# Moving squares of x and weight staging to later blocks in a planned matrix product on one core

## The chip, the cores and the metric

One core of a Trainium2 chip runs the whole program. The metric is device time in microseconds (us) of one execution; the time given for a kernel is the median of its runs. Five engines take instructions in their own order: TensorE (PE), VectorE (DVE), ScalarE (ACT), GpSimd (POOL) and SyncE (SP). POOL, SP and, at the start and the end, ACT also issue DMA transfers.

## The reference

```python
batch, m, k, h, n = 16, 512, 768, 3072, 768      # x, w1, b1, w2 are float32
y = np.maximum(np.matmul(x, w1) + b1, 0)
return np.matmul(y, w2).astype(np.float32)
```

So 8192 rows of x go through a 768 to 3072 layer with bias and relu, and then through a 3072 to 768 layer.

## The kernel before

The rows are cut into 8 blocks of 1024 (`NSB`), the 3072 hidden columns into two halves (`NCH`). An iteration `it` takes one block through one half: `it` 0 to 7 are the first pass over the blocks with the first half of w1 and w2, `it` 8 to 15 the second pass. The second pass begins with the block that ended the first one (`block`), and adds its result to what the first pass has stored in the output: POOL's DMA stores accumulate.

Each iteration has a first stage, the product of x and w1 (`add_first`, matmuls at L924), and a second stage, the product of y and w2 (`add_second`, matmuls at L1045). Both use a bilinear scheme with fewer products than the plain one: 20 products replace 24 in each of the two column groups of the first stage, 20 replace 24 in the second. The price is sums of inputs on DVE: of x (`X_SUMS`, L674), of w1 (`W1_SUMS`, L690, over both column groups `g` at once), of y (L897) and of w2 (`W2_SUMS`, L712). It also costs operations behind the products: they are kept as sums in `s`, seed another PSUM bank, or go out. In the first stage these are on ACT (L954, L958) and DVE (L961, L964, L970), in the second on ACT (L1057) and DVE (L1060). Block 0 alone has a plain first product (`first_block`, L834), since its weights' sums aren't there yet; its first rows are turned by PE.

The second stage makes eight outputs per block, each in one of the four buffers `o`, and stores each as 384 KB. Normally an output with a kept sum `u` is added to it on DVE. In the iterations named in `APART` it is not: ACT copies the output alone, SP stores the kept sum (L1093, in the first pass), and POOL's accumulating store (L1090) adds the output to it in DRAM.

x reaches `xn` by a POOL load with a cast to fp16 (L571, two halves of 768 KB per block), and SP's DMA transposes (L625, eight per block) bring it into `x`. In the last iteration the free slots of `x` hold what the first pass stored (`prior`, L1019); POOL adds the kept sums to it (L1098), and DVE then adds the product.

The fast scheme is only used for data in a known range, so the kernel sums squares of all inputs: of x in place in `xn` after the transposes (L633, ACT), of block 0's first four row tiles from `o` (L1197), of w1 (L728) and w2 (L742). `add_check` compares them in the second pass; a general path follows if they are out of range.

The weights of the second half are staged by POOL into DRAM in fp16, in the first pass: six strips of w1 (L553, `w1d`) and twelve of w2 (L559, `w2d`), three per iteration from `it` 1 on. SP loads them when pass 1 ends.

The order on every engine is made before the program runs, by `Graph.run`: each step is a task with an engine, a cost in ns, a latency and the data it reads and writes. PE's order is the order in which its tasks are added. The other engines take, of what can start, the task with the earliest due time, worked out backward from the PE task that needs it. Tasks marked `idle`, all squares among them, go into gaps that the plan shows. `take` picks the PSUM bank, kept-sum slot or output buffer. On the chip each engine then runs its list strictly in order and waits at each step for what that step reads or overwrites.

```python
self.g.add("ACT", 1030, square, writes=[("xn", s), ("stat", "x", i)], due=due, idle=True)   # add_square_x
to = it + 2 + (it + 2 == NSB)      # iteration_end: the block after the next is loaded into xn
```

Of the kernel before, what the change touches and what calls it, by code (L numbers as in the profile page):

```python
# [14 lines left out]
ACTF = mybir.ActivationFunctionType  # L15
# [215 lines left out]
class Graph:  # L231
# [65 lines left out]

        return self.places["ps"][i ^ 1][0] <= start

    def take(self, reg, start):  # L300

        p = self.places[reg.kind]
        if reg.kind == "ps":
            if reg.seeded:
                found = sorted((max(f, start), self.spare(i, start), -full, i)
                               for i, (f, full) in enumerate(p)
                               if full >= (2 if reg.seeded == 2 else 1))
            else:
                found = sorted((max(f, start), self.spare(i, start), full, i)
                               for i, (f, full) in enumerate(p))  # L310
            if reg.n == 2:
                at = {i: f for f, _, _, i in found}
                found = sorted((max(f, at[i + 1]), i) for i, f in at.items()
                               if i % 2 == 0 and i + 1 in at)
                if not found or found[0][0] > 1e8:
                    return None
                f, i = found[0]
                return f, [i, i + 1]
            if not found or found[0][0] > 1e8:
                return None  # L320
            return found[0][0], [found[0][3]]
        best = None
        step = reg.n if reg.kind == "s" else 1
        for i in range(0, len(p) - reg.n + 1, step):
            f = max(p[k][0] for k in range(i, i + reg.n))
            if f < 1e8 and (best is None or f < best[0]):
                best = (f, list(range(i, i + reg.n)))
        return best

    def run(self, begin=0.0, lookahead=0.2, ahead=5):  # L330
# [6 lines left out]
        for t in reversed(self.tasks):  # L337
# [4 lines left out]
            due = t.late = late  # L342
# [5 lines left out]
        product = {}  # L348
        for t in self.tasks:
            if t.engine == "PE":  # L350
                for r in t.regs:
                    product.setdefault(r, t.pe)
        avail = {e: [] for e in self.ENGINES}
        free = {e: begin for e in self.ENGINES}
        order, head, drift, left = [], 0, 0.0, len(self.tasks)
# [11 lines left out]
        while left:  # L367
            best = None
            for e in self.ENGINES:
                cands = []  # L370
                low = 1e9
                for t in avail[e]:
                    if e == "PE" and t.pe != head:
                        continue
                    start = max(free[e], t.ready)
                    if start > low + lookahead:
                        continue
                    ok = True
                    for r in t.regs:
                        if r.at is None:  # L380
                            if e != "PE" and r.kind == "ps" and r in product:
                                if product[r] > head + ahead:
                                    ok = False
                                    break
                            got = self.take(r, start)
                            if got is None:
                                ok = False
                                break
                            start = max(start, got[0])
                    if not ok:  # L390
                        continue
                    if t.idle and start < t.due + drift:
                        d = demand[e]
                        while first[e] < len(d) and d[first[e]].end is not None:
                            first[e] += 1
                        if first[e] < len(d) and start + t.ns > d[first[e]].late + drift + 0.3:
                            continue
                    cands.append((start, t))
                    low = min(low, start)
                if cands:  # L400
                    start, t = min((c for c in cands if c[0] <= low + lookahead),
                                   key=lambda c: (c[1].due, c[1].n))
                    if best is None or (start, t.n) < best[:2]:
                        best = (start, t.n, t, e)
# [50 lines left out]

APART = (0, 7)

STATS = ((1, 2, 3, 4, 5, 6, 7), (2, 3, 4))  # L460


class Fast:
# [153 lines left out]
        return x[:, :, (s % 2) * P:(s % 2 + 1) * P]  # L617

    def add_load_x(self, it, half):
        self.g.add("POOL", 760, lambda: self.load_x(it, half), lat=9.0,  # L620
                   writes=[("xn", 4 * half + s) for s in range(4)])

    def add_turns(self, it):
# [3 lines left out]
                writes=[("x", 2 * (s // 2) + k, s % 2) for k in range(2)])  # L627

    def add_square_x(self, it, s, due=None):
        i = it * 8 + s  # L630

        def square():
            self.nc.scalar.activation(out=self.xn[:, s, :], in_=self.xn[:, s, :],  # L633
                                      func=ACTF.Square,
                                      accum_out=self.stat[:, self.stat_at["x"] + i:][:, 0:1])
        self.g.add("ACT", 1030, square, writes=[("xn", s), ("stat", "x", i)], due=due, idle=True)
# [43 lines left out]

    def add_w1_sums(self):

        for o, i, j, sign in W1_SUMS:
            a, b, d = (self.w1s[q] for q in (o, i, j))

            def add(a=a, b=b, d=d, sign=sign):
                w = self.v1.rearrange("p g a k h -> p g a (k h)")
                self.nc.vector.tensor_tensor(out=w[:, :, a], in0=w[:, :, b], in1=w[:, :, d],  # L690
                                             op=ALU.add if sign > 0 else ALU.subtract)
            self.g.add("DVE", 950, add,
                       reads=[("w1", g, q) for g in range(2) for q in (b, d)],
                       writes=[("w1", g, a) for g in range(2)])

    def add_w2_signs(self, c):
        for i in W2_NEG:
# [2 lines left out]
                out=self.v2[:, a], in_=self.v2[:, a], func=ACTF.Copy, scale=-1.0),  # L700
                writes=[("w2", a, s) for s in range(4)])

    def add_w2_sums(self, c, parts):
        slot = self.w2s[c]
        for n, (o, i, j, sign) in enumerate(W2_SUMS):
            a, b, d = (slot[q] for q in (o, i, j))
            for s0 in range(0, 4, 4 // parts):
                s1 = s0 + 4 // parts

# [313 lines left out]
    def add_second(self, it):  # L1023
# [71 lines left out]
                **({"accum_op": ALU.add} if c else {}))  # L1095

        def add_prior(to, u, b):
            nc.gpsimd.tensor_tensor(out=self.prior(to), in0=self.prior(to), in1=sum_of(kept[u]),  # L1098
                                    op=ALU.add if b > 0 else ALU.subtract)

        where = {p: ch for ch, chain in enumerate(SECOND_CHAINS) for k, p in chain if k == "m"}
        for kind, n in steps:
# [14 lines left out]
            if what == "out":  # L1117
                dest = Reg("o")
                if final:
                    engine = "DVE"  # L1120
                    if u is not None:
                        self.g.add("POOL", 1850, lambda to=to, u=u, b=b: add_prior(to, u, b),
                                   reads=self.prior_keys(to) + [kept[u]],
                                   writes=self.prior_keys(to))
                    reads += self.prior_keys(to)
                elif u is not None and apart:
                    assert b == 1
                    self.g.add("POOL" if c else "SP", 1375 if c else 100,
                               lambda to=to, u=u: store_sum(to, u), reads=[kept[u]],
                               writes=[("out", self.block(it), to)], lat=6.5)  # L1130
                    engine = "ACT"
                elif u is not None:
                    reads.append(kept[u])
# [12 lines left out]
            if what == "out" and not (final and n == last):  # L1146
# [1 line left out]
                self.g.add("SP" if plain else "POOL", 100 if plain else 1375,  # L1148
                           lambda to=to, dest=dest, plain=plain: store(to, dest, plain),
                           reads=[dest],  # L1150
                           writes=[("out", self.block(it), to)], lat=6.5)

# [37 lines left out]
    def plan(self):  # L1192
        g, NSB, NIT = self.g, self.NSB, self.NIT
        self.presets()
        for s in range(4):
            def square(s=s):
                self.nc.scalar.activation(out=self.junk, in_=self.o[:, s],  # L1197
                                          func=ACTF.Square,
                                          accum_out=self.stat[:, self.nsum + s:][:, 0:1])
            self.first_rows = getattr(self, "first_rows", [])  # L1200
            self.first_rows.append(square)
        self.hold = [g.held(Reg("o"), [s]) for s in range(4)]
        self.first_block()
        for s in range(4):
            g.add("ACT", 1030, self.first_rows[s], reads=[("rows", s), self.hold[s]],
                  writes=["junk", ("stat", "x", s)], idle=True, due=24.0)
        for s in range(4):
            self.add_square_x(0, 4 + s)
        self.add_stats(0, False, second=False)
        self.add_w2_signs(0)  # L1210
        self.add_stats(0, False, first=False)
        self.add_w2_sums(0, 2)
        self.add_w1_sums()
        self.add_load_x(1, 1)
        self.iteration_end(0)
        later = None
# [10 lines left out]
    def iteration(self, it):  # L1227
# [6 lines left out]
        if it == NSB - 1:  # L1234
# [4 lines left out]
                    reads=[("w1d", gi, h) for h in range(3)],  # L1239
                    writes=[("w1", gi, a) for a in range(6)])  # L1240
            self.add_stats(1, False, second=False)
            self.add_w1_sums()
        if it <= 6:
            for n in range((it - 1) * 3, it * 3):
                gi, h = divmod(n, 3)
                if n < 6:
                    g.add("POOL", 850, lambda gi=gi, h=h: self.load_strip(self.w1dram, 1, gi, h),
# [6 lines left out]
    def iteration_end(self, it):  # L1254
# [4 lines left out]
        self.add_second(it)  # L1259
        if it + 1 < NIT and it + 1 != NSB:  # L1260
            self.add_turns(it + 1)
            if it + 1 < NSB:
                for s in range(8):
                    self.add_square_x(it + 1, s)
            to = it + 2 + (it + 2 == NSB)
# [4 lines left out]
        if it == NSB - 1:  # L1270
# [6 lines left out]
                    writes=[("w2", slot[i], s) for s in range(4)])  # L1277
            self.add_w2_signs(1)
            self.add_stats(1, False, first=False)
            self.add_w2_sums(1, 2)  # L1280

    def build(self):
        self.place_all()
# [62 lines left out]
```

## Time and profile before

| | us |
|---|---|
| median of 3 runs | 875.39 |
| lowest and highest | 875.18, 876.65 |
| the profiled execution: its time | 876.98 |
| the profiled execution: its span, first to last instruction | 875.3 |
| PE busy in it | 855.2 |
| DVE, ACT, POOL busy | 686.8, 478.9, 143.2 |
| mean granted clock of TensorE | 0.994 |

The profile is of one execution. A row of the page or of an answer names the line of the kernel, the engine, the operation and what it writes and reads. Idle time is given with what ended it, as `[3.38 <-DMA out_dram<-o]`: the engine had been idle for 3.38 us when a store of `o` let it go on. In the list of waits the three numbers are us in total, times, and the longest. In a table of stretches each row has the stretch, its length, and the busy time of PE, PEld (weight loads, which run beside matmuls), DVE, ACT and POOL with their instructions, then TensorE's granted clock, the share of the 16 DMA engines and GB/s. An SP or POOL row that issues a transfer lasts as long as the issue; its landing is told apart.

### The profile page before, as it was taken

How to read it: one execution, taken by the hardware profiler on the slowest of the kernel's cores; microseconds unless marked ns; L12 is line 12 of the kernel's file. 1: busy time of each engine (PE TensorE's matmuls, PEld its weight loads, DVE VectorE, ACT ScalarE, POOL GpSimd, SP SyncE). 2: the span in 40 equal slices, each digit the busy share in tenths (PEclk: the TensorE clock that was granted, in tenths of full speed). 3: DMA queues.
4: the chain of work that ended last, by engine and by line, in shares of the span. 5: the costliest groups of instructions: out<-in, count | busy, mean ns of one | idle time of the engine just before them, and what ended most of it. 6: DMA issues, size and time to landing. Idle time of an engine off the chain costs nothing.

```text
span 875.3 us, 16234 instructions
## 1 busy us (share of the span) xinstructions
PE 855.2 (98%) x6445; PEld 635.0 (73%) x6445; DVE 686.8 (78%) x1023; ACT 478.9 (55%) x951; POOL 143.2 (16%) x155
## 2 busy tenths in 40 slices
PE   8998799999999999999999999999999999999996
PEld 8556568778686776868678686877868677686873
DVE  2787497887879788797999979788786978869774
ACT  6876456757476583654755253664737435253350
POOL 5213010100101001000030402213031130402204
PEclk9999899999999999999999999999999999999998
DMA  9979977484835649372698868779586886963743
GB/s 211 192 162 207 132 135 168 89 214 74 184 106 107 165 73 243 59 159 74 232 211 136 128 102 126 116 126 151 105 122 106 133 127 109 139 98 55 127 145 127
DMA packets 162978, 119.85 MB, mean 137 GB/s; under 512 B 93244, under 2 KB 161364, under 8 KB 162644
## 3 DMA queue, kind: packets, MB, share of 16 engines
q0 software_dynamic: 49760, 58.99, 44.3%
q1 hardware_dynamic: 112672, 58.81, 27.5%
q8 instruction: 51, 0.84, 0.4%
q10 hardware_dynamic: 468, 1.00, 0.3%
q14 instruction: 27, 0.22, 0.1%
HBM read 73.94 MB, written 59.77 MB: 153 GB/s over the span
## 4 chain that ended last, share of the span: by engine, by line
PE 88%; DMA 4%; issue 4%; DVE 1%; POOL 1%; ACT 1%; SPq 0%; POOLq 0%; DVEq 0%; ACTq 0%
PE ps L924 42%; PE ps L1045 42%; PE ps L834 4%; DMA out_dram<-o 1%; DMA x<-xn 1%; POOL x L1098 1%; DMA out_dram<-s 1%; DVE v L690 1%; PE ps L776 1%; DMA o<-in_x_dram 1%; DVE s L1060 0%; DMA x<-out_dram 0%; ACT s L958 0%; DVE ps L1060 0%; ACT junk L728 0%
## 5 line engine op out<-in xcount | busy, mean ns | idle before, releaser
L1045 PE MATMUL ps<-v,y 128*128 128x384 f16 x2560 | 419.3, 326 | 1.1 <-DVE o L1060 0.6
L924 PE MATMUL ps<-x,v 128*128 128x256 f16 x3600 | 398.5, 273 | 10.0 <-ACT ps L958 6.1
L924 PEld LDWEIGHTS <-v 128*128 128x128 f16 x3600 | 353.1, 98 | 54.4 <-issue 11.1
L1045 PEld LDWEIGHTS <-y 128*128 128x128 f16 x2560 | 250.4, 98 | 165.8 <-issue 2.0
L961 DVE CUSTOM_DVE_ANT_0 y<-ps,s 128x512 f16<-128x512 f32 x240 | 161.4, 688 | 72.7 <-PE ps L924 53.7
L897 DVE TENSOR_TENSOR y<-y 128x1024 f16<-128x1024 f16 (+2 forms) x227 | 165.6, 755 | 8.7 <-ACT y L843 6.2
L958 ACT ACTIVATE s<-ps,bt 128x256 f32<-128x256 f32 x180 | 73.8, 472 | 109.9 <-PE ps L924 106.6
L1090 POOL DMA_DIRECT2D out_dram<-o x68 | 81.8, 1297 | 201.3 <-DVE o L1060 68.3
L674 DVE TENSOR_TENSOR x<-x 128x768 f16<-128x768 f16 (+1 forms) x168 | 109.5, 684 | 0.5
L571 POOL DMA_DIRECT2D xn<-in_x_dram x30 | 22.7, 758 | 474.1 <-ACT xn L633 303.3
L1057 ACT ACTIVATE ps<-ps 128x768 f32<-128x768 f32 x48 | 38.2, 795 | 108.9 <-PE ps L1045 90.4
L1057 ACT ACTIVATE s<-ps 128x768 f32<-128x768 f32 x64 | 51.7, 809 | 61.9 <-PE ps L1045 61.3
L958 ACT ACTIVATE y<-ps,bt 128x256 f16<-128x256 f32 x180 | 73.6, 471 | 20.2 <-PE ps L924 18.4
L633 ACT ACTIVATE xn<-xn 128x768 f16<-128x768 f16 x60 | 50.2, 838 | 9.5 <-DMA x<-xn 9.3
L1060 DVE TENSOR_TENSOR o<-ps,s 128x768 f32<-128x768 f32 x52 | 49.1, 954 | 7.5 <-PE ps L1045 4.1
L1057 ACT ACTIVATE o<-ps 128x768 f32<-128x768 f32 x42 | 33.9, 808 | 21.5 <-PE ps L1045 13.5
L1060 DVE TENSOR_TENSOR s<-ps,s 128x768 f32<-128x768 f32 x32 | 30.6, 956 | 14.3 <-PE ps L1045 13.7
L970 DVE TENSOR_TENSOR s<-s,ps 128x512 f32<-128x512 f32 x30 | 20.5, 684 | 20.1 <-PE ps L924 20.1
L958 ACT ACTIVATE ps<-ps,bt 128x256 f32<-128x256 f32 x60 | 26.9, 448 | 17.1 <-PE ps L924 8.1
L954 ACT ACTIVATE ps<-ps 128x512 f32<-128x512 f32 x60 | 35.0, 584 | 0.7
L834 PE MATMUL ps<-x,v 128*128 128x256 f16 (+1 forms) x216 | 31.9, 308 | 0.3 <-DVE x L784 0.3
L1060 DVE TENSOR_TENSOR o<-s,ps 128x768 f32<-128x768 f32 x26 | 24.7, 950 | 7.8 <-DMA out_dram<-o 6.8
(63 smaller groups left out, 367.6 us busy)
## 6 DMA issues: line engine op xcount, KB each, us to landing
out_dram<-o POOLq DMA_DIRECT2D x68, 384.0 KB, 6.8
out_dram<-o SPq DMA_DIRECT2D x59, 384.0 KB, 6.0
xn<-in_x_dram POOLq DMA_DIRECT2D x28, 768.0 KB, 8.3
out_dram<-s SPq DMA_DIRECT2D x12, 384.0 KB, 8.2
x<-out_dram SPq DMA_DIRECT2D x8, 384.0 KB, 3.4
v<-in_w_dram POOLq DMA_DIRECT2D x6, 384.0 KB, 9.1
v<-in_w_dram POOLq DMA_DIRECT2D x12, 192.0 KB, 10.1
w1d<-in_w_dram POOLq DMA_DIRECT2D x6, 384.0 KB, 14.7
```

Of the source, the lines that this page charges most:

```text
L633: self.nc.scalar.activation(out=self.xn[:, s, :], in_=self.xn[:, s, :], func=ACTF.Square, accum_out=self.stat[:, self.stat_at["x"] + i:][: ...
L674: self.nc.vector.tensor_tensor(out=self.two(x, out), in0=self.two(x, in0), in1=self.two(x, in1), op=ALU.add if sign > 0 else ALU.subtract)
L834: nc.tensor.matmul(self.ps[:, ps.at[0], cols], lhsT=self.v1[:, gi, 2 * h + k2, k, j * P:(j + 1) * P], rhs=rhs, start=(k2 == 0 and k == 0), ...
L897: self.nc.vector.tensor_tensor(out=self.two(y, out), in0=self.two(y, in0), in1=self.two(y, in1), op=ALU.add if sign > 0 else ALU.subtract)
L924: nc.tensor.matmul(self.ps[:, at, j * self.QM:(j + 1) * self.QM], lhsT=self.v1[:, gi, self.w1s[FIRST_V[p]], k, j * P:(j + 1) * P], rhs=sel ...
L954: nc.scalar.activation(out=out, in_=ps, scale=float(a), func=func if kind == "out" else ACTF.Copy)
L958: nc.scalar.activation(out=out[:, halves[j]], in_=ps[:, halves[j]], func=func, scale=float(a), bias=beta(j))
L961: nc.vector._custom_dve(TENSOR_ADD_SAT, out=out, in0=ps, in1=s, s0=F_MAX, s1=0.0)
L1045: nc.tensor.matmul(self.ps[:, bank[ch].at[j], 0:NH], lhsT=self.y[:, self.ys[SECOND_U[p]], m0:m0 + P], rhs=self.v2[:, slot[SECOND_V[p]], s, :],
L1057: nc.scalar.activation(out=out, in_=ps, func=ACTF.Copy, scale=float(a))
L1060: engine.tensor_tensor(out=out, in0=in0, in1=in1, op=ALU.add if a == b else ALU.subtract)
L1090: nc.gpsimd.dma_start(out=rows, in_=out, accum_op=ALU.add)
```

## The change

- Block 0 leaves `APART`, so its kept sums are added on DVE and it has plain stores.
- The squares of x of blocks 0 and 1 are no longer made in the first pass; they are made when those blocks come again in the second pass (`it` 9 and 10, in the iteration before each). The special squares at L1197 go.
- w1's sums for block 1 are made for each column group by itself (two adds of 768 columns for one of 1536), and the last four w2 sums of the first half are made whole instead of in two parts.
- The staging of the second half's weights begins at `it` 2 with four strips per iteration.
- In the last block the kept sums are added to `prior` on DVE.
- The planner gets other latencies for x loads and for block 0's stores, prefers a clean PSUM bank for a chain that is not seeded, and lets no other engine take a bank that an earlier chain of products still needs.

```diff
+    def take(self, reg, start, but=()):
...
-                found = sorted((max(f, start), self.spare(i, start), full, i)
-                               for i, (f, full) in enumerate(p))
+                found = sorted((max(f, start), self.spare(i, start) + (full > 0), full, i)
+                               for i, (f, full) in enumerate(p) if i not in but)
...
+        chains, opened = sorted(product, key=product.get), 0
...
                             got = self.take(r, start)
+                            if got is not None and e != "PE" and r.kind == "ps":
+                                while chains[opened].at is not None:
+                                    opened += 1
+                                c = chains[opened]
+                                if product[c] < product[r] and not self.take(c, start, got[1]):
+                                    got = None
...
-APART = (0, 7)
+APART = (7,)
+W2_WHOLE = (4, 0)
...
-        self.g.add("POOL", 760, lambda: self.load_x(it, half), lat=9.0,
+        self.g.add("POOL", 760, lambda: self.load_x(it, half), lat=13.0,
...
-        i = it * 8 + s
+        i = self.block(it) * 8 + s
...
-    def add_w1_sums(self):
+    def add_w1_sums(self, groups):
+        n = len(groups)
...
-                w = self.v1.rearrange("p g a k h -> p g a (k h)")
+                w = self.v1[:, groups[0]:groups[0] + n].rearrange("p g a k h -> p g a (k h)")
...
-            self.g.add("DVE", 950, add,
+            self.g.add("DVE", 950 if n == 2 else 552, add,
...
-    def add_w2_sums(self, c, parts):
+    def add_w2_sums(self, c, whole=12):
...
+            parts = 1 if n + whole >= len(W2_SUMS) else 2
...
-            nc.gpsimd.tensor_tensor(out=self.prior(to), in0=self.prior(to), in1=sum_of(kept[u]),
+            nc.vector.tensor_tensor(out=self.prior(to), in0=self.prior(to), in1=sum_of(kept[u]),
...
-                        self.g.add("POOL", 1850, lambda to=to, u=u, b=b: add_prior(to, u, b),
+                        self.g.add("DVE", 955, lambda to=to, u=u, b=b: add_prior(to, u, b),
...
-                               writes=[("out", self.block(it), to)], lat=6.5)
+                               writes=[("out", self.block(it), to)], lat=9.0 if it == 0 else 6.5)
...
         self.first_block()
-        for s in range(4):
-            g.add("ACT", 1030, self.first_rows[s], reads=[("rows", s), self.hold[s]],
-                  writes=["junk", ("stat", "x", s)], idle=True, due=24.0)
-        for s in range(4):
-            self.add_square_x(0, 4 + s)
...
-        self.add_w2_sums(0, 2)
-        self.add_w1_sums()
+        self.add_w2_sums(0, W2_WHOLE[0])
+        for gi in range(2):
+            self.add_w1_sums((gi,))
...
-        if it <= 6:
-            for n in range((it - 1) * 3, it * 3):
+        if 2 <= it <= 6:
+            for n in range((it - 2) * 4, min((it - 1) * 4, 18)):
...
-            if it + 1 < NSB:
+            if (it + 1 < NSB) == (self.block(it + 1) > 1):
                 for s in range(8):
                     self.add_square_x(it + 1, s)
```

## The prediction

> **What bounds the kernel now.** The page first: TensorE (PE) is busy for nearly the whole span, so a change of order can only win back the little that PE idles or runs slowly.
>
> ```profile
> PE   855.2 (98%) x6445; PEld 635.0 (73%) x6445; DVE 686.8 (78%) x1023; ACT 478.9 (55%) x951; POOL 143.2 (16%) x155
> ```
>
> Then PE's own waits, to see where the other 20 us lie (5.7 us are the start, 6.7 us the end after the last matmul):
>
> ```profile
> PE ps L924 <- ACT ps L958: 6.1, 1, 6.1
> PE ps L924 <- ACT o L1057: 2.8, 2, 1.9
> PE ps L924 <- ACT ps L954: 0.6, 1, 0.6
> PE ps L1045 <- DVE o L1060: 0.6, 1, 0.6
> ```
>
> The first three stand in one stage, the first product (L924) of block 1. Busy time by stage shows it: the second product of block 0, the first of block 1, the first of block 2 (undisturbed), the last block's second product.
>
> ```profile
> 44.28:70.28 26.00, 26.00 (x161) 15.65 (x160) 23.04 (x42) 16.87 (x29) 3.91 (x4) 1.00 0.84 176
> 70.28:108.88 38.60, 29.00 (x242) 24.34 (x240) 22.72 (x36) 22.54 (x50) 7.29 (x7) 0.91 0.99 163
> 135.04:161.24 26.20, 26.20 (x242) 23.44 (x240) 18.35 (x30) 19.32 (x44) 0.00 (x0) 1.00 0.64 135
> 841.27:868.60 27.33, 26.48 (x162) 15.55 (x159) 18.22 (x22) 6.01 (x9) 9.69 (x6) 1.00 0.27 95
> ```
>
> The same 240 matmuls take 38.60 us in block 1 and 26.20 us in block 2. Why is in ACT's timeline:
>
> ```profile
> 70.77 0.81 ACT L1057 ACTIVATE o<-ps 128x768 f32<-128x768 f32 x1 [3.38 <-DMA out_dram<-o]
> 74.16 0.81 ACT L1057 ACTIVATE o<-ps 128x768 f32<-128x768 f32 x1 [1.84 <-DMA out_dram<-o]
> 77.21 0.81 ACT L1057 ACTIVATE o<-ps 128x768 f32<-128x768 f32 x1 [1.52 <-DMA out_dram<-o]
> 99.88 0.84 ACT L633 ACTIVATE xn<-xn 128x768 f16<-128x768 f16 x1 [7.54 <-DMA x<-xn]
> ```
>
> At 70 to 77 us ACT copies block 0's outputs and waits for one of the four `o` buffers, whose accumulating store waits for the store of the kept sum (8.33 us, then 10.57 us on the chain that ended last). At 92 us ACT comes to a square of x (L633) and waits for the transposes of the same rows; they start at 89.54, beside three w1 staging loads issued at 83.4 to 85.1, and land 7.7 to 10.3 us after issue where undisturbed ones take 2.8. ACT's bias evictions (L958) stand behind both, and PE needs their banks: 1.91+0.93+0.57+6.08 = 9.49 us of idle PE. After the last wait 42 matmuls take 6.63 us where 42 x 0.1092 (26.20/240) = 4.59 would do, with the granted clock at 0.68 between 100 and 110 us: 2.05 us more.
>
> **Part by part.** PE's program is unchanged, instruction for instruction; DVE, ACT, POOL and SP get another order.
>
> Block 0 no longer apart. Gone: six stores of kept sums; six accumulating stores on POOL become plain ones on SP, so that eight plain stores share the four buffers, as in blocks 1 to 6. Six output copies (0.81) leave ACT, six adds (0.955, L1060) go to DVE, as in block 1's second stage (109.04 to 135.04, no PE wait). This takes the first three waits away. What is late next is DVE: 23.04 busy of 26.00, plus 6 x 0.955 = 5.73, minus three w1 sums of 0.95 that leave this stage, 25.9: full. Going through its new order with PE's releases, the last output add ends 2.8 us after block 1's first stage starts (1.4 in block 2's); PE, taking a bank every 0.655 us from two free ones, asks for that bank at about 3.9. Cover 1.1 us, each us beyond it costs one.
>
> Squares of blocks 0 and 1. Sixteen activations of about 1.03 (0.84 and a 0.19 accumulator read) leave the first 60 us of ACT. Block 2's x loads then wait for block 1's transposes alone (POOL waited 25.92 us for L633, until 56.93). Block 2's squares stay where the 7.54 us wait was, but staging w1 is gone from beside their transposes, which by then meet only plain stores issued by about 73: landing 2.8 as at 150.1, where the same square waited for nothing. So the fourth wait and its slow matmuls go too. With both, block 1's first stage is block 2's: 38.60 - 26.20 = 12.40 us. Bounds: 3.4 (only the first waits go) to 12.4; I take 12.4, since the undisturbed stage has the same instructions around it.
>
> The sixteen return in the second pass, one block ahead of repeats 9 and 10, at the place in ACT's order that pass 1 uses. ACT is busy 14.66 of 26.20 there (501 to 527), so time is no matter; waiting is. The first square comes 17.9 us into a stage, the transposes start at 15.1 and land after 2.7 (463.97) and 4.3 (516.17): one wait of 1.5 us, about what ACT can hide (7.54 of wait gave 6.08 of PE idle). I put 0.3, bounds 0 and 4.
>
> w1 staging: four loads instead of three, one block later, behind block 3's x loads. In block 2's second half they start near 109 and at 21.7 (the longest landing of such a load) end by 134; the next transposes start near 138. Nothing. The x loads of the second pass stand between accumulating stores (1.2 each on POOL) and have over 20 us to land. Nothing.
>
> w1 sums by group: 24 of 0.55 for 12 of 0.95, 1.8 us more DVE work, and four w2 sums whole (0.95 for two of 0.55) give 0.6 back. Nine of the first group go to 13.5 to 21 us, where DVE waited 5.08 and 1.18 us. The third strip lands at 4.8 + 8.9 = 13.7; seven sums at 0.53 and the table end near 17.8, and the x copy that PE waits for was at 18.73. Cover 0.9. The new bank rules of the planner show only in DVE's order, above all at the switch to the second half of the weights (422.64 to 448.87: DVE 25.27 busy of 26.23, PE already 0.23 late). I put 0.2 for all such slips, bounds 0 and 3.
>
> [...] POOL's load issues beside two-input DVE sums: 0.70 to 0.71 at 21.1 and 22.1 us under y sums, 0.75 at 28.00 under a w1 sum, as without them; only the w1 staging at 83.4 took 2.3 where 0.81 is usual. [...]
>
> Last block: six adds (1.80 each) leave POOL and become 0.955 on DVE (L1060's rows; from PSUM, the nearest). Before:
>
> ```profile
> 862.49 7.11 POOL L1098 TENSOR_TENSOR x<-x,s 128x768 f32<-128x768 f32 x4 [4.63 <-DVE s L1060]
> 866.10 2.73 DVE L1060 TENSOR_TENSOR o<-ps,x 128x768 f32<-128x768 f32 x3 [3.69 <-POOL x L1098]
> 869.63 1.02 DVE L1060 TENSOR_TENSOR o<-x,ps 128x384 f32<-128x384 f32 x2 [0.80 <-POOL x L1098]
> ```
>
> DVE waited 3.69 + 0.80 for POOL, and PE 0.25 + 0.57 behind it. In the new order DVE, from the sum released 19.5 us into the stage, has one sum, four prior adds, three outputs and two halves: 19.5 + 8 x 0.9 + 1.0 and some 0.6 of waiting = 28.3, against 29.4 before: 1.1 saved. But SP now issues a whole 384 KB store behind the last half store: 0.35 later, landing 2.5 to 4.2 instead of 3.5. Net 0.6 saved, bounds -0.4 and 1.5.
>
> Sum on the profiled execution: 876.98 (span 875.30 and 1.68 around it) - 12.40 - 0.60 + 0.30 + 0.20 = 864.48. It lies 1.59 above the median 875.39, so the median forecast is 862.9.
>
> **Rivals.** Changes under 0.2% (1.75 us) can hardly be told from none here.
>
> First, DVE takes over the wait: block 0's second stage is full on DVE, and if 3 us more spill than the 1.1 us cover, PE waits 3: about 866. For it: 25.9 of 26.0. Against: the next stage has 4.75 us of w1 sums shrunk to five of 0.53.
>
> [...]
>
> Third, the late transposes were x loads' and stores' doing and not w1's: the square's wait stays, 6.08 + 2.05 = 8.1 given back, 871.0. For it: DMA share stays 0.6 to 1.1 there. Against: blocks 2 to 6 load and store as much and their first stages stay at 26.20.
>
> Fourth, slower: the stall moves with the squares. In the second pass the transposes run beside accumulating stores; if they land as late as at 89.54 (10.3), ACT waits 7.5 and PE loses 8.1, twice, 16.2: about 879. It turns slower than before by 1.75 when the two reach 7.3 each (12.8 + 1.75, halved), a wait of 6.7 with its slow matmuls, a landing near 9.5. Measured there: 2.7 and 4.3, at most 6.1 for late ones.
>
> Fifth, the change does not do it: the `o` waits return on DVE, which carries more of PE's work than ACT, because plain stores land late too (block 1's took up to 8.5, before's sums 11.9). Then both stalls stay in other names: 875.
>
> **Numbers.** Forecast 0.60; first 0.13, second 0.08, third 0.10, fourth 0.04, fifth 0.05 (of it 0.01 slower). Low end: 875.39 - 12.4 - 1.5 - 0.3 for PE's small waits elsewhere = 861.2. High end 868.0: the first rival with the second-pass bound half spent. That holds the forecast and the first two, 0.81. Faster 0.60+0.13+0.08+0.10 = 0.91, same 0.04, slower 0.05.
>
> **What would show it.** Right: block 1's first stage near 26.2 with clock 1.00, no ACT wait on `out_dram` there and none over 2 us on L633's transposes; no POOL adds at the end and PE's last stage near 26.3. Wrong: a PE wait on DVE between 60 and 80 or before 25 us, ACT waiting for transposes near 464 or 516 less the gain, or a span that ends later after the last matmul than 6.7 us by more than a us.

## The result and the profile after

The changed kernel takes 863.9 us (median; runs from 863.6 to 865.36) where the kernel before took 875.28 in the same comparison (875.14 to 876.65). The ratio is 0.987, with a 95% interval of 0.9853 to 0.9887: faster by 1.3%. The profiled execution took 863.6 us, with a span of 862.1.

The page's first row and the longest waits of PE, after (us in total, times, longest):

```profile
PE 850.1 (99%) x6445; PEld 631.4 (73%) x6445; DVE 699.0 (81%) x1043; ACT 475.1 (55%) x945; POOL 125.2 (15%) x143
```

```profile
PE ps L601 <- DVE ones L542: 1.3, 1, 1.3
PE ps L787 <- DMA o<-in_x_dram: 0.6, 1, 0.6
PE ps L845 <- DMA v<-in_w_dram: 0.6, 1, 0.6
PE ps L935 <- DVE o L1071: 0.5, 1, 0.5
```

The three waits of the first product (now L935) on ACT are gone. PE's busy time fell too, by 5.1 us with the same instructions: slow matmuls of block 1 (29.00 us of PE in its first stage, now 26.23) and of the start (below) are gone as well. The same four stages as before, in the trace after (start and end, length, busy PE, PEld, DVE, ACT and POOL, granted clock, DMA share, GB/s):

```profile
42.70:68.70 26.00, 26.00 (x162) 15.66 (x161) 23.75 (x39) 9.61 (x13) 1.48 (x2) 1.00 0.90 193
68.70:94.93 26.23, 26.23 (x242) 23.47 (x240) 22.58 (x38) 18.99 (x44) 0.00 (x0) 1.00 0.43 92
120.93:147.13 26.20, 26.20 (x242) 23.48 (x240) 18.41 (x30) 19.18 (x44) 0.00 (x0) 1.00 0.73 148
828.22:854.40 26.18, 26.16 (x162) 15.56 (x159) 22.68 (x27) 6.01 (x9) 0.00 (x0) 1.00 0.30 103
```

Block 1's first stage takes 26.23 us instead of 38.60, at full clock. DVE in block 0's second stage is at 23.75 of 26.00, not at 25.9; the last of the six output adds falls into the next stage. ACT in block 1's first stage shows no wait for a store. Its first square of x (L641) still stands for 1.12 us, for which its row names no releaser: the first of its transposes, issued at 84.0, lands 3.8 us later, just before the square starts. PE doesn't wait behind it:

```profile
70.21 0.84 ACT L969 ACTIVATE s<-ps,bt 128x256 f32<-128x256 f32 x2 [3.94 <-PE ps L935]
82.65 0.84 ACT L969 ACTIVATE s<-ps,bt 128x256 f32<-128x256 f32 x2 [1.95 <-PE ps L935]
87.81 0.84 ACT L641 ACTIVATE xn<-xn 128x768 f16<-128x768 f16 x1 [1.12 <-issue]
```

The gain is followed by the lead of the trace after over the trace before at stage marks: 1.58 us at the second stage of block 0; 13.95 after block 1's first stage; 13.83 at the end of the first pass; 12.98 after the third stage of the second pass (the first product of `it` 9); 14.19 at the last matmul; 13.20 at the end of the span.

The 1.58 of the start are no part of the change. Of them 0.32 are a first landing of x that came later in the trace before (5.71 for 5.39). Most of the rest lies in the 24 transposing matmuls of the first x rows, 5.26 us from the first to the last in the trace before, 3.33 in the one after and 3.24 to 3.59 in all others (a wait of 0.58 us for weights gives part of this back). The trace before, then the one after:

```profile
5.71 5.26 PE L776 MATMUL ps<-ident,o 128*128 128x128 f32 x24 [0.64 <-DMA o<-in_x_dram]
```

```profile
5.39 1.50 PE L787 MATMUL ps<-ident,o 128*128 128x128 f32 x12 [0.65 <-DMA o<-in_x_dram]
7.22 1.50 PE L787 MATMUL ps<-ident,o 128*128 128x128 f32 x12 [0.34 <-DVE x L795]
```

In every other profile of this study, with or without the change, block 0's second stage starts at 42.5 to 43.1 us, in that of before alone at 44.28. This fits the 1.59 by which the profiled execution of before lay above its median; there is no second profile of before that could show it.

The losses: in the second stage of the second pass an output add on DVE waits for a store, and PE for that add (DVE's timeline, then PE's):

```profile
486.71 0.96 DVE L1071 TENSOR_TENSOR o<-ps,s 128x768 f32<-128x768 f32 x1 [0.98 <-DMA out_dram<-o]
```

```profile
487.73 26.56 PE L935 MATMUL ps<-x,v 128*128 128x256 f16 x240 [0.48 <-DVE o L1071]
```

And at the end DVE works on after PE's last matmul (854.38):

```profile
848.98 2.69 DVE L1109 TENSOR_TENSOR x<-x,s 128x768 f32<-128x768 f32 x3
...
851.77 0.96 DVE L1071 TENSOR_TENSOR o<-ps,x 128x768 f32<-128x768 f32 x1
852.64 0.95 DVE L1109 TENSOR_TENSOR x<-x,s 128x768 f32<-128x768 f32 x1
853.68 1.82 DVE L1071 TENSOR_TENSOR o<-ps,x 128x768 f32<-128x768 f32 x2
855.42 1.01 DVE L1071 TENSOR_TENSOR o<-x,ps 128x384 f32<-128x384 f32 x2
...
856.46 0.34 SPq L1087 DMA_DIRECT2D out_dram<-o  x1
856.85 0.83 SPq L1099 DMA_DIRECT2D out_dram<-o  x1
```

PE's last stage is 1.14 us shorter (26.16), but the span ends 7.72 us after the last matmul, 0.99 later than before: DVE has no idle time between 848.98 and 856.43.

### The profile page after: what moved, and what is told of

It reads as the page before. It is cut to its first block, busy times and chain, and to the rows that moved or that the text cites. A ratio compares the mean times of both kernels' runs of the same rounds, so it can differ in the third digit from the quotient of the medians.

```text
span 862.1 us, 16228 instructions
## 1 busy us (share of the span) xinstructions
PE 850.1 (99%) x6445; PEld 631.4 (73%) x6445; DVE 699.0 (81%) x1043; ACT 475.1 (55%) x945; POOL 125.2 (15%) x143
## 5 line engine op out<-in xcount | busy, mean ns | idle before, releaser
L935 PE MATMUL ps<-x,v 128*128 128x256 f16 x3600 | 396.1, 273 | 0.9 <-DVE o L1071 0.5
L935 PEld LDWEIGHTS <-v 128*128 128x128 f16 x3600 | 352.2, 98 | 44.0 <-issue 1.7
L1101 POOL DMA_DIRECT2D out_dram<-o x62 | 74.4, 1275 | 178.2 <-DMA out_dram<-s 60.8
L1071 DVE TENSOR_TENSOR o<-ps,s 128x768 f32<-128x768 f32 x56 | 52.9, 954 | 8.9 <-PE ps L1056 4.7
L641 ACT ACTIVATE xn<-xn 128x768 f16<-128x768 f16 x64 | 53.5, 838 | 3.9 <-DMA x<-xn 2.5
L1068 ACT ACTIVATE o<-ps 128x768 f32<-128x768 f32 x36 | 29.0, 809 | 12.1 <-PE ps L1056 12.0
L1071 DVE TENSOR_TENSOR o<-s,ps 128x768 f32<-128x768 f32 x28 | 26.6, 949 | 7.2 <-DMA out_dram<-o 6.1
```

The source lines that it names most:

```text
L935: nc.tensor.matmul(self.ps[:, at, j * self.QM:(j + 1) * self.QM], lhsT=self.v1[:, gi, self.w1s[FIRST_V[p]], k, j * P:(j + 1) * P], rhs=sel ...
L1068: nc.scalar.activation(out=out, in_=ps, func=ACTF.Copy, scale=float(a))
L1071: engine.tensor_tensor(out=out, in0=in0, in1=in1, op=ALU.add if a == b else ALU.subtract)
L1101: nc.gpsimd.dma_start(out=rows, in_=out, accum_op=ALU.add)
```

## The experiments

Twelve kernels, on four chips; before's median on them was 875.06 to 875.98. "Stage" is block 1's first stage, 38.60 us before and 26.23 after.

| kernel | us | ratio, interval | stage |
|---|---|---|---|
| 1 plain outputs of block 0 alone | 872.14 | 0.9953 [0.9937, 0.997] | 35.15 |
| 2 staging alone | 868.15 | 0.9915 [0.9885, 0.9944] | 30.65 |
| 3 squares alone, with bank rules | 875.8 | 0.9992 [0.9971, 1.0013] | 37.36 |
| 4 after, three w1 loads held back | 867.83 | 0.9902 [0.987, 0.9935] | 26.87 |
| 5 plain outputs and staging | 870.61 | 0.9942 [0.9926, 0.9959] | 33.17 |
| 6 plain outputs and sums by group | 866.29 | 0.99 [0.9883, 0.9916] | 29.08 |
| 7 after, with whole w1 sums | 866.55 | 0.9903 [0.9886, 0.992] | 28.99 |
| 8 after, last adds on POOL | 864.87 | 0.9876 [0.9859, 0.9892] | 26.74 |
| 9 after, last whole store first | 864.51 | 0.9872 [0.9856, 0.9889] | 26.92 |
| 10 as 9, one pair of adds on POOL | 864.28 | 0.9872 [0.9855, 0.9888] | 26.75 |
| 11 after, block 0 apart | 867.79 | 0.9918 [0.9902, 0.9935] | 30.49 |
| 12 plain outputs, staging, sums by group | 865.32 | 0.9886 [0.987, 0.9903] | 26.99 |

**1. Plain outputs of block 0 alone** (on the kernel before).

```diff
-APART = (0, 7)
+APART = (7,)
```

> The kernel before, with block 0 treated as blocks 1 to 6 are (only the last block apart): no kept sum of block 0 is stored, its eight outputs leave as plain stores on SP. Squares, staging of w1, w1 sums and the end stay as before. Theory A (all of the 12.4 us comes from block 0's accumulating stores on POOL: they hold the output buffers, and they hold the three w1 staging loads back until these lie beside block 2's transposes): the loads now follow the x loads of block 2 near 59 us, both stalls go, block 1's first stage takes 26.2 to 26.5 us, the time is 863.0 to 864.5. Theory B (each part of the change has its share; this one gives the first three waits only, 1.91+0.93+0.57 = 3.41): the stage takes 35.2, the time is 871.9.

The time is theory B's, but not by its mechanism. ACT's waits for stores are gone, and so is the 7.5 us wait of the square (1.78 is left; POOL issued the three w1 loads at 58.23 already). PE waits for DVE instead. PE's timeline, then DVE's:

```profile
72.46 1.47 PE L924 MATMUL ps<-x,v 128*128 128x256 f16 x12 [0.19 <-DVE o L1060]
74.98 2.78 PE L924 MATMUL ps<-x,v 128*128 128x256 f16 x24 [1.05 <-DVE s L964]
80.10 0.83 PE L924 MATMUL ps<-x,v 128*128 128x256 f16 x6 [2.34 <-DVE x L674]
82.28 17.24 PE L924 MATMUL ps<-x,v 128*128 128x256 f16 x132 [1.35 <-DVE x L674]
```

```profile
64.13 1.94 DVE L690 TENSOR_TENSOR v<-v 128x1536 f16<-128x1536 f16 x2
...
67.47 0.96 DVE L1060 TENSOR_TENSOR o<-ps,s 128x768 f32<-128x768 f32 x1 [0.53 <-DMA out_dram<-o]
...
71.45 0.95 DVE L1060 TENSOR_TENSOR o<-s,ps 128x768 f32<-128x768 f32 x1 [0.91 <-DMA out_dram<-o]
...
77.10 3.41 DVE L674 TENSOR_TENSOR x<-x 128x768 f16<-128x768 f16 x6
```

DVE does two wide w1 sums (L690) amid block 0's outputs, and its sums of x run until 82 us, where PE already needs them. It is busy for 29.47 us in a stage that should take 26.2. This is the prediction's first rival, at three times its price, in a kernel without the grouping of w1's sums that the prediction had counted in: 35.15 - 26.20 = 8.95 us, of it 5.46 idle (with 0.53 for ACT) and the rest slow matmuls (granted clock 0.62 from 80 to 84 us, 0.53 from 84 to 88).

**2. Staging alone** (on the kernel before).

```diff
-        if it <= 6:
-            for n in range((it - 1) * 3, it * 3):
+        if 2 <= it <= 6:
+            for n in range((it - 2) * 4, min((it - 1) * 4, 18)):
```

> The kernel before, with only the staging of w1 moved as in the change (one block later, four loads a block). Theory A: the transposes of block 2 meet no w1 load, the 7.5 us wait of the square and the slow matmuls go (6.08+2.05 = 8.1), the waits for the output buffers (3.4) stay: block 1's first stage 30.5, the time 867.2. Rival C (the transposes are late because of the accumulating stores issued at 78 to 85 us, or of x loads): the square waits as long as before, stage 38.6, time 875.3. Between the two, a wait shortened in part says that both share the transposes' delay.

Theory A: 38.60 - 30.65 = 7.95 us of the stage go. The transposes land 2.8 us after issue (median), although four accumulating stores are issued at 77.85 to 83.8 as before; of the square's 7.54 us wait 0.35 is left:

```profile
70.11 0.81 ACT L1057 ACTIVATE o<-ps 128x768 f32<-128x768 f32 x1 [3.68 <-DMA out_dram<-o]
73.36 0.81 ACT L1057 ACTIVATE o<-ps 128x768 f32<-128x768 f32 x1 [1.71 <-DMA out_dram<-o]
76.41 0.81 ACT L1057 ACTIVATE o<-ps 128x768 f32<-128x768 f32 x1 [1.51 <-DMA out_dram<-o]
104.74 0.84 ACT L633 ACTIVATE xn<-xn 128x768 f16<-128x768 f16 x1 [0.35 <-DMA x<-xn]
```

**3. Squares alone** (on the kernel before, with the planner's bank rules of the change).

```diff
-        i = it * 8 + s
+        i = self.block(it) * 8 + s
...
-        for s in range(4):
-            g.add("ACT", 1030, self.first_rows[s], ...)
-        for s in range(4):
-            self.add_square_x(0, 4 + s)
...
-            if it + 1 < NSB:
+            if (it + 1 < NSB) == (self.block(it + 1) > 1):
```

> The kernel before, with only the squares of blocks 0 and 1 moved to the second pass, and with the planner's new bank rules, without which this order cannot be planned. Block 0 stays apart and w1 is staged where it was. Theory A: block 1's first stage keeps both stalls, 38.6 to within 1.5 us, and the time is 874.5 to 877 (squares in the second pass cost 0 to 1). Rival D (ACT, loaded with sixteen squares in the first 60 us, is what makes copies, and so stores and loads, late): the stage falls below 33, the time below 870.

Theory A: no difference that can be measured. The w1 loads are still issued beside the transposes (79.90), the square waits 5.06 us and PE stands 3.60:

```profile
96.72 0.84 ACT L640 ACTIVATE xn<-xn 128x768 f16<-128x768 f16 x1 [5.06 <-DMA x<-xn]
```

The stage gains 1.24, and the second and third stages of the second pass lose 2.29 (27.39 and 27.10 for 26.00 and 26.20). The ten runs of this kernel spread from 871.79 to 878.48, so its one profile is one draw of the stalls.

**4. Three w1 loads put beside transposes** (on the changed kernel).

```diff
+            if it == 3:
+                g.add("POOL", 100, lambda: self.nc.gpsimd.tensor_copy(
+                    out=self.mark, in_=self.y[:, 8, 0:1]), reads=self.y_keys(8, 0), writes=["mark"])
-            for n in range((it - 2) * 4, min((it - 1) * 4, 18)):
+            for n in ((), (), (0, 1, 2), (3, 4, 5), (6, 7, 8, 9), (10, 11, 12, 13), (14, 15, 16, 17))[it]:
...
+                          reads=["mark"] if it == 3 else [],
```

> The changed kernel, with three of the six w1 staging loads held back: a copy of one column on POOL reads a y operand of block 3's first stage (ready near 10.9 us into it), and the loads follow it, so that they lie beside block 4's transposes, which start 15.1 us into that stage, as in block 1's first stage of the kernel before. Theory A (w1 loads beside transposes delay them, ACT stands in its order at the square, PE waits for ACT's evictions): transposes land 7 to 10 us after issue instead of 2.8, a square waits 4 to 7.5 us, block 3's first stage takes 29 to 34 instead of 26.2, time 867 to 872. Rival C (not w1's loads): stage 26.2, time 863.9.

Theory A: block 3's first stage takes 30.34 us where it took 26.20. POOL's issue, ACT's wait and PE's behind it, and PE's clock then (same columns as the table of stages):

```profile
185.09 2.44 POOL L561 DMA_DIRECT2D w1d<-in_w_dram  x3
```

```profile
195.74 0.84 ACT L641 ACTIVATE xn<-xn 128x768 f16<-128x768 f16 x1 [3.50 <-DMA x<-xn]
```

```profile
198.28 6.41 PE L935 MATMUL ps<-x,v 128*128 128x256 f16 x42 [2.31 <-ACT ps L969]
```

```profile
200.00:204.50 4.50, 4.50 (x30) 3.48 (x29) 2.64 (x4) 2.64 (x8) 0.00 (x0) 0.68 0.00 0
```

Here the loads were put back without the apart block, the first pass's squares of blocks 0 and 1 or the wide sums, and the stall came with them, 42 slow matmuls included. The eight transposes landed 2.8 to 6.2 us after issue (median 4.4), less than forecast, and the square's wait lies below the forecast too; the late ones decide.

**5. Plain outputs and staging** (the first two edits together; DVE's order is that of the first).

> The kernel with block 0's outputs plain (the first experiment), and the staging of w1 moved as in the change; DVE's order is the same as in the first experiment, where block 1's first stage took 35.15 us and PE waited for DVE (x sums L674 3.69, L964 1.05). Theory F (DVE has too much to do between block 0's outputs and block 1's x sums; where the loads lie is no matter): the stage stays at 34 to 35.2, time 871 to 872. Theory G (three w1 loads issued at 58 us beside the plain stores make these land late, and DVE's adds wait for their buffers 0.53+0.69+0.91 = 2.13): the stage falls to 31 or less, time 868 or less.

Between the two: the stage falls by 1.98. DVE's waits for stores shrink from 0.53+0.69+0.91 to 0.57+0.16, so the w1 loads of 58 us did delay plain stores, but PE's waits of 2.34 and 1.35 us for x sums are the same. The backlog is the larger part.

**6. Plain outputs and sums by group** (on the first experiment).

```diff
-        self.add_w1_sums()
+        for gi in range(2):
+            self.add_w1_sums((gi,))
```

> The kernel with block 0's outputs plain, and the w1 sums of the start in two groups (24 of 0.55 for 12 of 0.95) as in the change; squares, staging and w2 sums as before. Theory F (the backlog on DVE): nine sums go to the waits of the first 21 us, two wide ones (1.9) leave block 0's second stage; block 1's first stage falls from 35.15 to 26.2 to 28, time 863 to 865. Theory G (w1 loads delay the stores): it stays above 32, time 869 or more.

The stage falls by 6.07 to 29.08. What stays are PE's 0.22 and 1.25, behind DVE adds that still wait 0.84+0.55+0.89 for stores, and 0.58 behind ACT, whose square waits 1.83 for its transposes. Theory F holds for the larger part. The stage misses its band (26.2 to 28) by the part that is theory G's; the twelfth experiment moves the w1 loads too.

**7. Whole sums in the changed kernel** (the reverse of the edit of the sixth).

> The changed kernel with one part undone: the w1 sums of the start are whole again (12 of 0.95), three of them inside block 0's second stage and four in block 1's first. Theory F: DVE's backlog returns, PE waits for x sums and output adds of DVE, block 1's first stage takes 29 to 35 us instead of 26.23, time 867 to 872. Theory G, or that the other parts are enough: stage 26.2 to 26.8, time 864 to 864.5.

Theory F, at the lower end: 28.99 for 26.23, with PE's waits on x sums back and no DVE wait for a store.

```profile
76.21 0.83 PE L935 MATMUL ps<-x,v 128*128 128x256 f16 x6 [0.81 <-DVE x L682]
78.39 19.46 PE L935 MATMUL ps<-x,v 128*128 128x256 f16 x174 [1.35 <-DVE x L682]
```

The time (866.55) lies below the 867 expected.

**8. The last block's adds on POOL** (in the changed kernel).

```diff
-            nc.vector.tensor_tensor(out=self.prior(to), ...
+            nc.gpsimd.tensor_tensor(out=self.prior(to), ...
```

> The changed kernel with one part undone: the six adds of kept sums in the last block are on POOL again. By the stage marks of the two traces this part gained PE 1.14 us in the last second product (27.30 to 26.16) and lost 0.99 after the last matmul (6.73 to 7.72). If those two belong to it, the last product takes 27.3 again, the span ends 6.7 after its last matmul, and the time is within 0.4 us of the changed kernel (863.8 to 864.3). If the prediction's 0.6 is right, 864.5. Rival: the longer end comes from something else, and the kernel loses the whole 1.1 (865.0).

The last product takes 27.3 again, but the span ends 6.95 after it. One profile says little here, so take all: from the start of the last product to the end of the span, the eight profiles with the adds on POOL (before and experiments 1, 2, 3, 5, 6, 8, 12) take 33.82 to 34.49, mean 34.14; the four with the adds on DVE and the same stores (after and 4, 7, 11) 33.21 to 33.89, mean 33.69. The part is worth about 0.45, with ranges that just overlap.

**9. The last whole store ahead of the half** (in the changed kernel: the task that makes and stores the two halves gets `after=` the store of the last whole output).

> The changed kernel with one order changed on SP: the last whole store goes ahead of the half store that it stood behind (issued 856.85, 0.83 long, landing at the end of the span). If that store sets the end: the span ends 4.6 after the half store's issue as in the kernel before, 861.1 instead of 862.1, the time 0.4 to 1.0 less than the changed kernel. If the last landing is set by DVE's halves alone: within 0.2.

The span ends 5.6 us after DVE's last half, as in the kernel after (5.67). But the half store's issue, now last, took 1.47 us instead of 0.34. So the order of these two stores alone gains nothing, and which landing sets the end is not shown.

**10. One pair of adds on POOL** (on the ninth).

```diff
+ON_POOL = (9,)
...
+            (nc.gpsimd if u in ON_POOL else nc.vector).tensor_tensor(
```

> The ninth experiment, and besides one pair of the adds of kept sums on POOL (1.8 us each, in parallel to DVE's 0.955). DVE is the last engine to finish here (three adds and an output end at 852.7, the halves at 856.43, 2 us after the last matmul at 854.38). If DVE sets the end, the halves end 0.9 to 1.0 us earlier and the span with them: 1.3 to 2.0 less than the changed kernel. If an output add then waits for POOL as in the kernel before (3.69 and 0.80 there), nothing or a loss up to 0.5 against the ninth.

No gain against the ninth. DVE lost two of its six adds, and the two that it kept at the end became longer, as did one of POOL's two (1804 and 2519 ns; groups of the last 9 us: busy, mean ns; DVE's by shape with min, median and max):

```profile
L1110 DVE TENSOR_TENSOR x<-x,s x2: 1522/1530/1539, 850.7 to 853.2; 128x768 f32<-128x768 f32 x2
```

```profile
L1110 POOL TENSOR_TENSOR x<-x,s 128x768 f32<-128x768 f32 x2 | 4.3, 2162 | 43.8 <-DVE s L1072 43.8
```

Alone they take 951 (DVE, kernel after) and 1804 (POOL, kernel before). No experiment made a kernel that beats the change.

**11. Block 0 apart in the changed kernel** (the reverse of the first edit).

> The changed kernel with one part undone: block 0 is apart again (six sums stored, accumulating stores on POOL). Squares, staging and sums stay as changed. In block 1's first stage, 26.23 us as changed: the waits for the output buffers return (3.4), the late transposes do not, since no w1 load lies near: 29.6 to 30.7 (30.65 with the staging alone), time 867.3 to 868.5. If the accumulating stores by themselves delay block 2's transposes: over 32, time over 869.5.

As expected: 30.49, from two waits of PE for ACT's copies, with the clock at 1.00.

```profile
71.61 1.47 PE L935 MATMUL ps<-x,v 128*128 128x256 f16 x12 [1.63 <-ACT o L1068]
74.88 24.28 PE L935 MATMUL ps<-x,v 128*128 128x256 f16 x216 [1.80 <-ACT o L1068]
```

**12. Plain outputs, staging and sums by group** (on the kernel before; edits 1, 2 and 6).

> The kernel before with block 0's outputs plain, the staging moved and the w1 sums by group; the squares of blocks 0 and 1, the w2 sums, the planner's bank rules and the last block's adds on POOL stay as before. Against the plain outputs with sums by group (block 1's first stage 29.08 us) it says what the staging is worth once DVE's backlog is gone: DVE's adds waited 0.84+0.55+0.89 there for stores to land, with three w1 loads beside them. Theory H (these waits, carried on by DVE, are PE's 1.25, 0.22 and 0.58): the stage falls to 26.2 to 27, time 863.5 to 864.5. Theory I (the squares of block 1 on ACT and their later x loads are what is left): it stays at 28 to 29, time 865.5 to 866.3.

The stage is theory H's, 26.99; the time is higher than it said. Two further things add to it: the last adds are on POOL (0.45), and block 0's second stage takes 26.57 for 26.00, with a PE wait of 0.41 for ACT, whose queue still holds block 1's squares there.

## Why the prediction was right, and where it was not

**The sum.** In the profiled execution 864.48 was predicted and 863.6 measured. Of the gain 1.58 is the slow start of before's profile; without it the time is 865.18, later than predicted and not earlier. The 1.59 taken off for the median was given no cause; by the marks it is that start. The median came out 863.9 for 862.9. Of this 1.0 the second pass is 0.55 and the end 0.45 (below); the 0.20 for slips did not show, since all other stages together differ by less than 0.1.

**Block 1's first stage: 12.40 predicted, 12.37 measured.** Four further kernels that share this stage's edits (4, 8, 9, 10) show 26.74 to 26.92, so 11.7 to 12.4 is the fairer reading. (Before's 38.60 is one profile too, of a kernel whose runs spread from 873.13 to 879.0.) What those four have more is a rest of the second stall: the first square stands 1.63 to 1.81 us there for 1.12, its first transpose lands 4.3 and 4.5 us after issue in the eighth and the ninth for 3.8, and PE waits 0.38 to 0.56 behind the square. Of the two stalls the second was explained rightly: staging alone took away 7.95 of a predicted 8.1, and put back beside transposes it made a stall. The third rival (x loads' and stores' doing) falls with both. Plain outputs ended ACT's three waits, as said.

**What the steps left unsaid: plain outputs pay only with the sums of w1 by group.** The prediction counted three w1 sums out of block 0's second stage, but it put the grouping among the slips (0.2 for all of them) and gave the end of the first stall to the plain outputs alone. Six adds moved to DVE without the grouping cost PE 8.95 us through DVE. The first rival had named this place, priced at 3 us. The w1 sums in two groups bring the stage from 35.15 to 29.08 without the staging and from 33.17 to 26.99 with it, and 2.76 come back when they are undone in the changed kernel. The last number is smaller for two reasons. PE's longest single wait is 2.34 us in the first and fifth kernels, with a clock down to 0.53 and 0.50 over four us after it, and 1.35 us in the seventh, where the clock stays at 1.00. And the first wait for x sums is 0.81 us there for 2.34 in the fifth; whether the squares, the bank rules or the whole w2 sums did that was not tried. Made by group, thirteen of the 24 sums are done by 28.4 us, where the kernel before starts its first wide one at 27.90, and none of them is left among the outputs. In the changed kernel the last output add ended 2.65 us into block 1's first stage (70.41 + 0.94 - 68.70) where 2.8 was predicted, so that step was right for the kernel as a whole.

**Squares.** Moved alone they gain nothing that can be measured. Between the twelfth and the eighth, which differ in the squares, the bank rules, the planner's latencies and four w2 sums, the ratios are 0.9886 and 0.9876 with overlapping intervals: block 0's second stage gains 0.57 (26.57 to 26.00), and the second pass loses 1.60.

**Second pass: 0.30 predicted, 0.85 measured** (26.65 and 26.40 for 26.00 and 26.20). The seven other profiles with moved squares show 0.80 to 2.29, the five others with squares in place (1, 2, 5, 6, 12) nothing. The size was too small, and the mechanism was half of it. In the second stage of the pass, which loses 0.65 (0.44 to 0.65 in the changed kernel's variants, 1.39 in the third), PE waits for DVE's output add, which waits for a store to land; the sum had no such term. Why the store is late there was not tried; POOL's x loads had moved behind the squares, among its accumulating stores, which is argued only. In the third stage the predicted wait is there. In the changed kernel, the seventh and the eleventh a square waits 1.29 to 1.36 us for its transposes, and no wait of PE behind it is listed. In 3, 4, 8, 9 and 10 it waits 1.73 to 2.04 us, and PE stands for 0.48 to 0.79 behind it (in 3, 8 and 10 the row names DVE's `y`, which ended together with ACT's eviction). ACT, then PE, in the ninth:

```profile
507.87 0.84 ACT L641 ACTIVATE xn<-xn 128x768 f16<-128x768 f16 x1 [1.73 <-DMA x<-xn]
```

```profile
510.41 4.74 PE L935 MATMUL ps<-x,v 128*128 128x256 f16 x42 [0.48 <-ACT ps L969]
```

In all five PE's wait is the square's less 1.25 us, and so it is in block 1's first stage (1.81 and 0.56 in the ninth, 1.83 and 0.58 in the sixth). ACT hides 1.25 us of such a wait (1.46 of the long ones of before and 3), where the prediction took 1.5. The fourth rival's 8.1 per block is far off.

**The end: 0.60 predicted, 0.15 between the two profiles, 0.45 over all of them.** The mechanism was right (no PE wait on POOL's adds), and DVE became the last engine as costed. The price of the whole store behind the half (0.35) was not shown: the ninth experiment moved it and gained nothing, with a longer issue of the half store.

**Second (0.08):** no run shows w1 sums that hold POOL's loads back: under them at 13.56 and 15.42 us an issue took 0.70 and 0.71, as elsewhere (0.70 and 0.71 in the kernel before). **Fifth:** no `o` wait returned in block 1.

## What to carry to other kernels

A wait that is taken off one engine is paid from another's slack, so test each part alone: here a part that looked incidental made the room that another part needed (block 1's first stage took 35.15 us without it, 29.08 with it). When an engine stands at a step in its order, look at what was put into the DMA queues beside the transfer that it waits for; moving the staging loads by one block was worth more here (868.15 us) than any other edit that was tried alone (872.14 and 875.8). And measure marks of equal stages in several profiles before giving a microsecond to a cause: the start alone differed by 1.6 us between executions.

## What the runs showed of the hardware

In these traces the cost of an idle piece of PE went with its length. Pieces of up to 1.91 us (before), 1.63 and 1.80 among them (11), left the clock at 1.00. Pieces of 2.31 (4) and 2.34 us (1 and 5) were each followed by a lower clock: 0.68 over 4.5 us in 4, 0.62 and 0.53 over four us each in 1, 0.50 over four us in 5. After one of 2.30 (3) the next 36 matmuls took 5.61 us, where 36 x 0.1092 = 3.93 would do. None between 1.91 and 2.30 was seen. In 3 and 4 no second piece follows within four us; in 5, shown here, one of 1.35 does, and the clock is at 0.50 for four us:

```profile
76.00:80.00 4.00, 1.29 (x7) 0.77 (x7) 3.62 (x7) 1.93 (x5) 0.00 (x0) 0.84 0.00 0
80.00:84.00 4.00, 3.02 (x15) 2.09 (x15) 2.85 (x6) 0.60 (x1) 0.00 (x0) 0.50 0.00 0
84.00:88.00 4.00, 4.00 (x32) 3.27 (x31) 2.58 (x4) 2.17 (x5) 0.00 (x0) 0.81 0.00 0
```

So the 2.31 us in the fourth experiment cost 4.14, and the 2.05 us in the sixth, in three pieces with a mean clock of 1.00 in the stage, 2.88. What makes the start 44.28 in one profile and 42.5 to 43.1 us in the others is not shown: the clock from 1 to 20 us is 1.00 in the four profiles where it was read (before, after, 3 and 6).

In the tenth experiment adds of two SBUF operands ran on DVE and POOL at the same time and took longer: DVE's two 1530 ns on average for 951, and the second of POOL's two 2519 for 1804. The four records fit adds that take turns: DVE's first starts at 850.69 and ends at 852.23, 0.8 us after POOL's first (849.61 to 851.4); POOL's second ends near 853.9, 1.7 us after that; DVE's second starts at 853.20 and ends at 854.72, 0.8 us after that. This is an estimate from four records, and spans on POOL are rough. DVE's adds with one operand in PSUM took 955 ns beside POOL's in the kernel before, and 955 without them in the kernel after. POOL's DMA issues beside DVE's w1 sums were no longer either (0.70 and 0.71 us, above).
